# Two feed-forward products of a decoder layer by seven products of quarters in place of eight

## The chip, the core and the metric
One core of a Trainium2 chip runs one program. The metric is device microseconds of one execution; lower is better.

## The reference
One layer over 1032 tokens (1024 of a prompt, 8 sampled), all in float32. Three head groups give `mix`; then

```
x = x + mix @ w_out                                   # 1024 x 1024
h2 = rms_norm(x, norm2_g)
x = x + square(relu(h2 @ w_ff1)) @ w_ff2              # 1024 -> 4096 -> 1024
```

## The kernel before
Features lie on the partitions, tokens along the free dimension. A float32 factor is split into a high part, rounded to the matmul's type, and a low part (`split`, lines 108 to 114: a cast on ACT, then a subtraction on DVE or POOL). `dense` (146 to 154) makes three matmuls of each 128-row tile: high by high, high by low, low by high. Tokens go in three groups of 344 (`TG`). `split`, `add`, `mul`, `sub` are helpers, so the profile shows DVE and POOL operations at L51, ACT's at L71 or L74, matmuls at L83, loads at L80.

`merge` (1168) loads the eight tiles of `mix` from memory and splits them. `out_proj` (1180) runs over eight output tiles `d`: one weight unit (`wunit`, two halves of 128x512), 72 matmuls, the residual added, the result stored to `x1s`, and its scaled, split form kept in `xg`; its squares are summed into `r2`. `ffn` (1211) takes `ff1(m)` for 32 tiles of the hidden layer (72 matmuls, relu, square, split into `hb`) and, after every fourth, `ff2(fb)`, which adds four hidden tiles' part to eight output tiles `ya`; the last round multiplies by `r2`, adds `x1s` and stores. So 64 units of 72 matmuls of 344 columns run there; each weight half is split by ACT and POOL, and results leave PSUM through DVE or ACT. The whole of the former `ffn` stands in the diff below with a minus.

A scheduler puts each engine's instructions in an order when the program is built; pools and their buffer counts decide what may run ahead. DMAs of these parts are issued by SP in its order.

## Time and profile before

| | us |
|---|---|
| three runs | 1544.86, 1545.30, 1550.38 |
| median | 1545.3 |
| profiled execution, span of its instructions | 1548.3 |
| PE busy in it | 1452.3 (94%) |
| DVE, ACT, POOL busy | 756.9, 459.7, 488.8 |

The page lists no time of the profiled execution beside its span, which lies 3.0 us above the median and within the three runs. Durations below are of that execution. A busy share says little by itself: what ends last in a stage is read from the chain and the waits there.

### The profile page before, as it was taken

The page shows a single profiled execution, that of the slowest core. Times are in us where ns is not written, and L with a number is a line of the kernel's source. Part 1 is how long each engine was busy: PE and PEld are TensorE (multiplying, and loading weights), DVE is VectorE, ACT ScalarE, POOL GpSimd, SP SyncE. Part 2 cuts the span into 40 slices and gives each one's busy share as a digit, 9 for nine tenths or more (in the row PEclk, how much of TensorE's full clock was granted, in tenths as well). Part 3 has the DMA queues.
Part 4 walks back from the last instruction along what each step waited for, and adds up shares of the span by engine and source line. Part 5 has one row for each costly group of instructions (what it writes and reads, how often), then busy time and mean ns, then how long its engine had stood idle before and what let it go on. Part 6 is the DMA issues. An engine that isn't in the chain of part 4 may idle for free.

```text
span 1548.3 us, 26824 instructions
## 1 busy us (share of the span) xinstructions
PE 1452.3 (94%) x10623; PEld 1348.1 (87%) x10623; DVE 756.9 (49%) x1690; ACT 459.7 (30%) x1012; POOL 488.8 (32%) x762
## 2 busy tenths in 40 slices
PE   5899899989898698898999999999999999999998
PEld 5888787879777467566999999999999999999998
DVE  7658467667757655875435203223232322323248
ACT  6433223223223143344433333131221312122130
POOL 7013574461242645440232222222221222222121
PEclk9899899899788577679999999999999999999999
DMA  6153323323435531237432111111111111111125
GB/s 232 60 171 114 91 67 104 98 62 109 125 105 127 156 77 43 82 98 252 153 121 82 55 41 50 47 46 51 41 55 41 48 49 41 55 41 49 48 66 180
DMA packets 102264, 136.87 MB, mean 88 GB/s; under 512 B 36115, under 2 KB 58604, under 8 KB 101996
## 3 DMA queue, kind: packets, MB, share of 16 engines
q1 hardware_dynamic: 96924, 128.61, 25.8%
q0 software_dynamic: 5216, 6.56, 2.0%
q8 instruction: 83, 1.36, 0.3%
q14 instruction: 41, 0.34, 0.1%
HBM read 102.07 MB, written 34.10 MB: 88 GB/s over the span
## 4 chain that ended last, share of the span: by engine, by line
PE 76%; DVE 8%; DMA 5%; POOL 5%; issue 3%; ACT 2%; SPq 1%; ACTq 0%; POOLq 0%; DVEq 0%
PE d L83 38%; PE g L83 33%; POOL inv L51 4%; PE cx L83 2%; PE cy L83 2%; DMA qs<-xs 2%; PE g L87 1%; SPq L80 1%; DVE F L51 1%; DMA mst<-mixs 1%; DMA W<-ws 1%; DMA ws<-inv 1%; DVE hbig L68 1%; DMA kn<-kvs 1%; DVE xs L68 0%
## 5 line engine op out<-in xcount | busy, mean ns | idle before, releaser
L83 PE MATMUL d<-xg,w 128*128 128x344 f32 x2304 | 366.1, 320 | 0.0
L83 PEld LDWEIGHTS d<-xg,w 128*128 128x128 f32 x2304 | 363.9, 188 | 0.9 <-ACT rel L71 0.3
L83 PE MATMUL g<-hb,w 128*128 128x344 f32 x2304 | 364.2, 320 | 0.0
L83 PEld LDWEIGHTS g<-hb,w 128*128 128x128 f32 x2304 | 363.1, 188 | 0.0
L51 POOL TENSOR_TENSOR w<-wf,w 128x512 fp32r<-128x512 f32 x130 | 169.6, 1305 | 553.5 <-ACT w L74 553.5
L83 PE MATMUL d<-hbig,w 128*128 128x344 f32 (+2 forms) x1296 | 227.7, 333 | 18.2 <-ACT w L74 9.5
L83 PEld LDWEIGHTS d<-hbig,w 128*128 128x128 f32 x1296 | 207.6, 205 | 33.0 <-ACT w L74 10.7
L74 ACT CAST w<-wf 128x512 fp32r<-128x512 f32 x190 | 117.5, 619 | 334.7 <-PE g L83 263.1
L51 DVE TENSOR_TENSOR ya<-g,ya 128x344 f32<-128x344 f32 x168 | 86.6, 515 | 187.4 <-PE g L83 187.3
L51 DVE TENSOR_TENSOR rel<-rel 128x344 f32<-128x344 f32 x96 | 49.5, 516 | 243.7 <-ACT rel L71 243.7
L71 ACT ACTIVATE rel<-d 128x344 f32<-128x344 f32 x96 | 43.9, 458 | 193.7 <-PE d L83 192.5
L51 DVE TENSOR_TENSOR hb<-rel,hb 128x344 fp32r<-128x344 f32 x96 | 70.9, 739 | 53.0 <-ACT hb L74 53.0
L51 POOL TENSOR_TENSOR inv<-inv,blk 128x54 f32<-128x54 f32 (+24 forms) x217 | 71.7, 330 | 53.8 <-DMA out_state_p<-sl 20.5
L51 POOL TENSOR_TENSOR inv<-inv,inv 128x54 f32<-128x54 f32 (+24 forms) x217 | 74.9, 345 | 15.9
L74 ACT CAST hb<-rel 128x344 fp32r<-128x344 f32 x96 | 46.0, 480 | 38.6 <-DVE rel L51 36.1
L51 DVE TENSOR_TENSOR w<-wf,w 128x512 fp32r<-128x512 f32 x60 | 42.3, 705 | 30.5 <-ACT w L74 29.6
L83 PE MATMUL d<-mix,w 128*128 128x344 f32 x288 | 51.2, 327 | 2.8 <-ACT mix L74 2.4
L83 PEld LDWEIGHTS d<-mix,w 128*128 128x128 f32 x288 | 45.9, 190 | 7.2 <-ACT mix L74 3.2
L51 POOL TENSOR_TENSOR r<-r,osq 128x344 f32<-128x344 f32 x21 | 24.5, 1170 | 86.2 <-ACT r L71 46.5
L71 ACT ACTIVATE xs<-pr,omm 128x344 f32<-128x344 f32 x42 | 24.5, 583 | 86.8 <-DVE pr L51 50.8
L83 PE MATMUL g<-mix,w 128*128 128x344 f32 x288 | 49.7, 323 | 0.0
L83 PEld LDWEIGHTS g<-mix,w 128*128 128x128 f32 x288 | 46.5, 190 | 0.2 <-issue 0.2
(370 smaller groups left out, 1861.2 us busy)
## 6 DMA issues: line engine op xcount, KB each, us to landing
wf<-in_w_ff SPq DMA_DIRECT2D x128, 256.0 KB
wf<-in_w_in SPq DMA_DIRECT2D x34, 256.0 KB
tmp<-xs SPq DMA_DIRECT2D x32, 256.0 KB
x<-in_xT SPq DMA_DIRECT2D x8, 516.0 KB
xs<-xs SPq DMA_DIRECT2D x24, 172.0 KB
xr<-in_xT SPq DMA_DIRECT2D x8, 516.0 KB
x1s<-xr SPq DMA_DIRECT2D x8, 516.0 KB
x<-x1s SPq DMA_DIRECT2D x8, 516.0 KB
```

The lines of the kernel that those rows point to most:

```text
L51: return (e or self.nc.vector).tensor_tensor(out, a, b, op=op)
L68: return self.nc.vector.scalar_tensor_tensor(out, a, s, b, op0=op0, op1=op1)
L71: return self.nc.scalar.activation(out, a, f, **k)
L74: return self.nc.scalar.copy(out, a)
L80: return self.nc.sync.dma_start(out=out, in_=a)
L83: return self.nc.tensor.matmul(out, l, r, start=start, stop=stop, **k)
L87: return self.nc.tensor.transpose(out, a, ident)
```

## The change
Both products are cut into quarters: hidden or output rows by halves, inner dimension by halves, tokens into two halves of 516 (`TH`), each of two groups of 258 columns (`TQ2`). Seven products of sums and differences of quarters (forms) give the four results. `w_forms` makes seven split forms of a unit's four raw 128x512 pieces: four DVE subtractions, seven casts on ACT, seven on POOL to finish the split. `x_early` and `x_late` make the token forms, `h_forms(c)` seven forms of 128x1032 from the hidden tiles, which now go to memory (`hs`) and come back. `product` has a PSUM tile of two banks, four in turn. `up(j, ws)` replaces `ff1` (16 steps of seven products of 24 matmuls), `down(c, o, ws, hf)` replaces `ff2` (8 rounds `c` of 4 outputs `o`, seven products of 12 matmuls each, added into six `acc` tiles). The weight forms have 7 buffers (tags `w`, `w2`), the hidden forms 8 (`xy`, `xe`), raw hidden tiles and their sums 8 (`t4`). `merge` and `out_proj` take `t4` tiles for their loads, and `out_proj` goes by pairs 0, 4, 1, 5 and so on. Some small constants lie in another pool.

```diff
+            self.ea = ctx.enter_context(pool("early_forms", L))
             with pool("mix", L) as self.fp:
                 self.merge()
                 self.out_proj()
-            with pool("ff", L) as self.fp:
-                self.ffn()
-            xgp.__exit__(None, None, None)
+            self.eb = ctx.enter_context(pool("late_forms", L))
+            psp.__exit__(None, None, None)
+            self.psp = ctx.enter_context(self.tc.tile_pool(name="psum2", bufs=2, space=PSUM))
+            self.ffn()
...
+    def t4(self):
+        return self.xgp.tile([128, T], F32, name=self.nm("t4"), tag="t4", bufs=8)
+    def hx(self, n=TH):
+        return self.ea.tile([128, TH], F32, name=self.nm("st"), tag="st", bufs=5)[:, :n]
...
-            f = self.fp.tile([128, TP], F32, name=self.nm("mst"), tag="mst", bufs=2)
-            self.dma(f, self.mixs[k])
+            f = self.t4()
+            self.dma(f[:, :TP], self.mixs[k])
...
-        for d in range(8):
+        self.x1 = [None] * 8
+        self.xf = [[None, None] for _ in range(7)]
+        for n, d in enumerate((0, 4, 1, 5, 2, 6, 3, 7)):
             w = self.wunit(I["w_out"][d])
-            xr = fp.tile([128, T], F32, name=self.nm("xr"), tag="xres", bufs=2)
+            xr = self.x1[d] = self.t4()
...
-            x = self.xgp.tile([128, 2, T], F32R, name=f"xg{d}")
-            self.split(x[:, 0], x[:, 1], xr, scale=v[:, V_G2 + d:V_G2 + d + 1])
-            self.xg.append((x[:, 0], x[:, 1]))
...
+            self.act(xr, xr, AF.Copy, scale=v[:, V_G2 + d:V_G2 + d + 1])
+            if n % 2:
+                self.x_early(n // 2)
...
+    def form(self, tile, k, x, e=None):
+        self.split(tile[:, 0, k], tile[:, 1, k], x, e=e)
+    def xt(self, i, half):
+        tag, n = (("xy", 4), ("xe", 4), ("xf", 6))[min(i // 2, 2)]
+        pool = self.ea if i < 4 else self.eb
+        self.xf[i][half] = pool.tile([128, 2, 2, TH], F32R, name=self.nm(tag), tag=tag, bufs=n)
+        return self.xf[i][half]
...
+    def x_early(self, k):
+        half = k // 2
+        b11, b12, b21, b22 = self.x_quads(k)
+        g = self.nc.gpsimd
+        if k % 2 == 0:
+            for i in range(4):
+                self.xt(i, half)
+        f = [self.xf[i][half] for i in range(4)]
+        self.form(f[0], k % 2, b11, g)
+        self.form(f[1], k % 2, b21, g)
+        t1 = self.hx()
+        self.sub(t1, b12, b11)
+        t2 = self.hx()
+        self.sub(t2, b22, t1)
+        self.form(f[2], k % 2, t2)
+        self.form(f[3], k % 2, t1)
+    def x_late(self):
+        g = self.nc.gpsimd
+        for i in (4, 5, 6):
+            for half in range(2):
+                self.xt(i, half)
+        f = lambda i, k: (self.xf[i][k // 2], k % 2)
+        for k in range(4):
+            b11, b12, b21, b22 = self.x_quads(k)
+            t3 = self.hx()
+            self.sub(t3, b22, b12)
+            self.form(*f(4, k), t3)
+        for k in range(4):
+            self.form(*f(5, k), self.x_quads(k)[3], g)
+        for k in range(4):
+            b11, b12, b21, b22 = self.x_quads(k)
+            u, t3 = self.hx(), self.hx()
+            self.sub(u, b21, b11)
+            self.sub(t3, b22, b12, g)
+            self.sub(u, u, t3)
+            self.form(*f(6, k), u)
+    def w_raw(self, src):
+        self.nwf = getattr(self, "nwf", 0) + 1
+        pool, tag, n = ((self.wp, "wf", 2), (self.eb, "wf2", 4))[self.nwf % 3 > 0]
+        raw = pool.tile([128, 512], F32, name=self.nm(tag), tag=tag, bufs=n)
+        self.dma(raw, src)
+        return raw
+    def w_form(self, x, e):
+        self.nwt = getattr(self, "nwt", 0) + 1
+        pool, tag, n = ((self.wp, "w", 4), (self.eb, "w2", 3))[self.nwt % 7 > 3]
+        w = pool.tile([128, 2, 512], F32R, name=self.nm(tag), tag=tag, bufs=n)
+        self.split(w[:, 0], w[:, 1], x, e=e)
+        return w
+    def w_forms(self, a11, a12, a21, a22):
+        g, v = self.nc.gpsimd, self.nc.vector
+        a11, a12, a21, a22 = (self.w_raw(x) for x in (a11, a12, a21, a22))
+        sx = lambda: self.hx(512)
+        r = [self.w_form(a11, g), self.w_form(a12, g)]
+        s1, s2 = sx(), sx()
+        self.add(s1, a21, a22, v)
+        self.sub(s2, s1, a11, v)
+        r += [self.w_form(s2, g), self.w_form(s1, g)]
+        s3 = sx()
+        self.sub(s3, a11, a21, v)
+        r.append(self.w_form(s3, g))
+        s4 = sx()
+        self.sub(s4, a12, s2, v)
+        return r + [self.w_form(s4, g), self.w_form(a22, g)]
+    def product(self, ws, xs):
+        out = self.psp.tile([128, 2, 512], F32, name=self.nm("pq"), tag="pq", bufs=4)
+        n = len(ws) * 3
+        for g in range(2):
+            i = 0
+            for (a, c), (hi, lo) in zip(ws, xs):
+                for l, r in ((a, hi), (a, lo), (c, hi)):
+                    self.mm(out[:, g, :TQ2], l, r[:, g * TQ2:g * TQ2 + TQ2], start=i == 0, stop=i == n - 1)
+                    i += 1
+        return out[:, :, :TQ2]
     def ffn(self):
-        nc, fp, I = self.nc, self.fp, self.I
-        hb = fp.tile([128, 6, 2, T], F32R, name="hb")
-        ya = fp.tile([128, 8, T], F32, name="ya")
-        def ff1(m):
-            w = self.wunit(I["w_ff1"][m], nc.gpsimd)
-            for t0, tn in TG:
-                p = self.ps("d")
-                self.dense(p[:, :tn], w, 0, self.xg, t0, tn)
-                r = fp.tile([128, 344], F32, name=self.nm("rel"), tag="rel", bufs=2)
-                self.act(r, p[:, :tn], AF.Relu)
-                self.mul(r, r, r)
-                self.split(hb[:, m % 6, 0, t0:t0 + tn], hb[:, m % 6, 1, t0:t0 + tn], r)
-        def ff2(fb):
-            last = fb == 7
-            hs = [(hb[:, m % 6, 0], hb[:, m % 6, 1]) for m in range(4 * fb, 4 * fb + 4)]
-            for dp in range(4):
-                w = self.wunit(I["w_ff2"][fb, dp], nc.gpsimd)
-                for d2 in range(2):
-                    d = dp * 2 + d2
-                    if last:
-                        x1 = fp.tile([128, T], F32, name=self.nm("x1"), tag="xres", bufs=2)
-                        self.dma(x1, self.x1s[d])
-                    for t0, tn in TG:
-                        p = self.ps("g")
-                        self.dense(p[:, :tn], w, d2 * 512, hs, t0, tn)
-                        y = ya[:, d, t0:t0 + tn]
-                        if fb == 0:
-                            self.cp(y, p[:, :tn])
-                        else:
-                            self.add(y, p[:, :tn], y)
-                        if last:
-                            self.mul(y, y, self.r2[:, t0:t0 + tn])
-                            self.add(y, y, x1[:, t0:t0 + tn])
-                    if last:
-                        self.dma(self.O["yT"][:, d], ya[:, d])
-        for fb in range(8):
-            for j in range(4):
-                ff1(fb * 4 + j)
-                if j == 0 and fb:
-                    ff2(fb - 1)
-        ff2(7)
+        nc, I = self.nc, self.I
+        two = lambda x: x.rearrange("p (g n) -> p g n", g=2)
+        self.hs = self.dp.tile([32, 128, T], F32, name="hs")
+        def up(j, ws):
+            xs = [[(f[k // 2][:, 0, k % 2], f[k // 2][:, 1, k % 2]) for k in range(4)] for f in self.xf]
+            w = [[(f[:, 0, k * 128:k * 128 + 128], f[:, 1, k * 128:k * 128 + 128]) for k in range(4)] for f in ws]
+            pp, h1, h2 = self.t4(), self.t4(), self.t4()
+            p1, u2, c11, c12, c21, c22 = (two(x[:, s * TH:s * TH + TH]) for x in (pp, h1, h2) for s in range(2))
+            def square(h, m):
+                self.stt(h, h, 0.0, h, ALU.max, ALU.mult)
+                self.mul(h, h, self.r2)
+                self.dma(self.hs[m], h)
+            p = self.product(w[0], xs[0])
+            self.cp(p1, p)
+            p = self.product(w[1], xs[1])
+            self.add(c11, p, p1)
+            p = self.product(w[2], xs[2])
+            self.add(u2, p, p1)
+            p5 = self.product(w[3], xs[3])
+            self.add(c12, p5, u2)
+            p = self.product(w[4], xs[4])
+            self.add(c21, p, u2)
+            self.add(c22, p5, c21)
+            p = self.product(w[5], xs[5])
+            self.add(c12, p, c12)
+            square(h1, j)
+            p = self.product(w[6], xs[6])
+            self.add(c21, p, c21)
+            square(h2, j + 16)
+        w1 = lambda j: self.w_forms(*(I["w_ff1"][m][:, i * 512:i * 512 + 512] for m in (j, j + 16) for i in range(2)))
+        w2 = lambda c, u: self.w_forms(*(I["w_ff2"][c, u, q] for q in range(4)))
+        ws = w1(0)
+        self.x_late()
+        for j in range(16):
+            nxt = w1(j + 1) if j < 15 else w2(0, 0)
+            if j == 15:
+                hf = self.h_forms(0)
+            up(j, ws)
+            ws = nxt
+        acc = [self.eb.tile([128, 4, TH], F32, name=f"acc{i}", tag="xf", bufs=6) for i in range(6)]
+        def down(c, o, ws, hf):
+            k0 = (o % 2) * 2
+            xs = [[(f[:, 0, k], f[:, 1, k]) for k in range(2)] for f in hf]
+            w = [[(f[:, 0, k * 128:k * 128 + 128], f[:, 1, k * 128:k * 128 + 128]) for k in range(k0, k0 + 2)] for f in ws]
+            c11, u2, u4, u3, p3, p4 = (x[:, o] for x in acc)
+            def to(out, p, first=True):
+                if c == 0 and first:
+                    self.cp(two(out), p)
+                else:
+                    self.add(two(out), p, two(out))
+            last = c == 7
+            g = nc.gpsimd
+            if c == 2 + o:
+                x1 = []
+                for d in (o, o + 4):
+                    x = self.t4()
+                    self.dma(x, self.x1s[d])
+                    x1 += [x[:, :TH], x[:, TH:]]
+                self.add(c11, c11, x1[0], g)
+                self.add(p4, p4, x1[2], g)
+                self.add(u4, u4, x1[3], g)
+                self.add(p3, p3, x1[1], g)
+                self.sub(p3, p3, x1[3], g)
+            put = lambda d, t, y: self.dma(self.O["yT"][:, d, t * TH:t * TH + TH], y)
+            p = self.product(w[0], xs[0])
+            to(c11, p)
+            to(u2, p)
+            p = self.product(w[1], xs[1])
+            to(c11, p, False)
+            if last:
+                put(o, 0, c11)
+            to(u2, self.product(w[2], xs[2]), False)
+            to(u4, self.product(w[3], xs[3]))
+            if last:
+                self.add(u4, u4, u2)
+                self.add(p3, p3, u4, g)
+                self.add(p4, p4, u2, g)
+            to(u3, self.product(w[4], xs[4]))
+            if last:
+                self.add(u4, u4, u3)
+                put(o + 4, 1, u4)
+                self.add(p4, p4, u3)
+            to(p3, self.product(w[5], xs[5]))
+            if last:
+                put(o, 1, p3)
+            to(p4, self.product(w[6], xs[6]))
+            if last:
+                put(o + 4, 0, p4)
+        for c in range(8):
+            for o in range(4):
+                if o % 2 == 0:
+                    nxt = w2(c, 1) if o == 0 else w2(c + 1, 0) if c < 7 else None
+                if o == 1 and c < 7:
+                    nhf = self.h_forms(c + 1)
+                down(c, o, ws, hf)
+                if o % 2:
+                    ws = nxt
+            if c < 7:
+                hf = nhf
+    def h_forms(self, c):
+        g, v = self.nc.gpsimd, self.nc.vector
+        q = []
+        wide = lambda: self.t4().rearrange("p (j n) -> p j n", j=2)
+        for f in range(2):
+            for t in range(2):
+                x = wide()
+                for j in range(2):
+                    self.dma(x[:, j], self.hs[f * 16 + 2 * c + j, :, t * TH:t * TH + TH])
+                q.append(x)
+        b11, b12, b21, b22 = q
+        r = []
+        def put(x, e):
+            n = c * 7 + len(r)
+            f = self.ea.tile([128, 2, 2, TH], F32R, name=self.nm("hf"), tag=("xy", "xe")[n % 8 // 4], bufs=4)
+            self.split(f[:, 0], f[:, 1], x, e=e)
+            r.append(f)
+        put(b11, g)
+        put(b21, v)
+        t1, t2, t3, t4 = (wide() for _ in range(4))
+        self.sub(t1, b12, b11, v)
+        self.sub(t2, b22, t1, v)
+        put(t2, g)
+        put(t1, v)
+        self.sub(t3, b22, b12, g)
+        put(t3, v)
+        put(b22, g)
+        self.sub(t4, b21, t2, v)
+        put(t4, v)
+        return r
```

Three places of the order. First DVE: before, in a round of `ff2` (`ya` the output sum, `g` a PSUM tile), only results out of PSUM, and an `ff1` square:

```order
L51 TENSOR_TENSOR ya_8636<-g_1637_12575,ya_8636 128x344
L51 TENSOR_TENSOR ya_8636<-g_1638_12589,ya_8636 128x344
L51 TENSOR_TENSOR ya_8636<-g_1639_12603,ya_8636 128x344
L51 TENSOR_TENSOR rel_1645_12652<-rel_1645_12652 128x344
L51 TENSOR_TENSOR hb_8635<-rel_1645_12652,hb_8635 128x344
```

Now, where `down(3, 3)` ends and `down(4, 0)` begins (`pq` a PSUM product, `acc` the sums, `t4` raw hidden tiles and their sums, `hf` a form, `st` a weight sum):

```order
L53 TENSOR_TENSOR t4_1936_14164<-t4_1931_14149,t4_1930_14146 128x1032
L53 TENSOR_TENSOR acc4_12466<-pq_1906_13982,acc4_12466 128x516
L53 TENSOR_TENSOR acc5_12467<-pq_1907_13996,acc5_12467 128x516
L53 TENSOR_TENSOR hf_1871_13673<-t4_1866_13656,hf_1871_13673 128x1032
L53 TENSOR_TENSOR st_1914_14024<-wf2_1910_14014,wf_1911_14016 128x512
L53 TENSOR_TENSOR t4_1937_14165<-t4_1933_14155,t4_1936_14164 128x1032
L53 TENSOR_TENSOR acc0_12462<-pq_1923_14047,acc0_12462 128x516
L53 TENSOR_TENSOR acc1_12463<-pq_1923_14047,acc1_12463 128x516
L53 TENSOR_TENSOR st_1915_14025<-st_1914_14024,wf_1908_14010 128x512
L53 TENSOR_TENSOR st_1918_14034<-wf_1908_14010,wf2_1910_14014 128x512
L53 TENSOR_TENSOR t4_1939_14167<-t4_1932_14152,t4_1937_14165 128x1032
L53 TENSOR_TENSOR acc2_12464<-pq_1926_14090,acc2_12464 128x516
```

Subtractions between SBUF tiles have come ahead of the results of `pq_1923`, the first product of the new round.

POOL, before, at any place of the feed-forward part:

```order
L51 TENSOR_TENSOR w_1623_12436<-wf_1622_12434,w_1623_12436 128x512
L51 TENSOR_TENSOR w_1631_12525<-wf_1630_12523,w_1631_12525 128x512
L51 TENSOR_TENSOR w_1633_12530<-wf_1632_12528,w_1633_12530 128x512
L51 TENSOR_TENSOR w_1641_12619<-wf_1640_12617,w_1641_12619 128x512
L51 TENSOR_TENSOR w_1643_12624<-wf_1642_12622,w_1643_12624 128x512
```

Now, over the same boundary: the seven splits `w`, `w2` of one weight set, with three splits `hf` and a subtraction of 1032 columns among and behind them:

```order
L53 TENSOR_TENSOR w_1883_13783<-wf2_1879_13775,w_1883_13783 128x512
L53 TENSOR_TENSOR hf_1867_13659<-t4_1864_13654,hf_1867_13659 128x1032
L53 TENSOR_TENSOR w_1884_13786<-wf_1880_13777,w_1884_13786 128x512
L53 TENSOR_TENSOR w_1887_13793<-st_1886_13790,w_1887_13793 128x512
L53 TENSOR_TENSOR w2_1888_13796<-st_1885_13789,w2_1888_13796 128x512
L53 TENSOR_TENSOR hf_1870_13669<-t4_1860_13644,hf_1870_13669 128x1032
L53 TENSOR_TENSOR w2_1890_13801<-st_1889_13799,w2_1890_13801 128x512
L53 TENSOR_TENSOR w2_1892_13806<-st_1891_13804,w2_1892_13806 128x512
L53 TENSOR_TENSOR w_1893_13809<-wf2_1882_13781,w_1893_13809 128x512
L53 TENSOR_TENSOR hf_1934_14158<-t4_1930_14146,hf_1934_14158 128x1032
L53 TENSOR_TENSOR t4_1938_14166<-t4_1933_14155,t4_1931_14149 128x1032
```

POOL's subtractions of 128x1032 now stand between weight splits, one of them ahead of the second weight form.

SP at the end of the sampled tokens' attention, before (`d4` its loads, `mst` the mixed tokens):

```order
L80 DMA d4_1128_7699<-in_mem_v 128x4x256
L80 DMA mst_1139_7773<-mixs_71 128x1024
L80 DMA d4_1129_7705<-in_mem_v 128x4x256
L80 DMA mst_1140_7777<-mixs_71 128x1024
L80 DMA d4_1130_7711<-in_mem_v 128x4x256
L80 DMA mst_1141_7781<-mixs_71 128x1024
```

Now:

```order
L82 DMA d4_1129_7705<-in_mem_v 128x4x256
L82 DMA mixs_71<-ao_1114_7640 128x512
L82 DMA d4_1130_7711<-in_mem_v 128x4x256
L82 DMA d4_1131_7717<-in_mem_v 128x4x256
L82 DMA t4_1134_7757<-mixs_71 128x1024
L82 DMA t4_1135_7761<-mixs_71 128x1024
```

The loads of the mixed tokens have moved behind the last load of that attention.

## Rows read from the trace of the kernel before

**Rows 1.** the profile's page: span, engine shares, PE and clock by slice.
```profile
span 1548.3 us, 26824 instructions
...
PE 1452.3 (94%) x10623; PEld 1348.1 (87%) x10623; DVE 756.9 (49%) x1690; ACT 459.7 (30%) x1012; POOL 488.8 (32%) x762
...
PEclk9899899899788577679999999999999999999999
...
GB/s 232 60 171 114 91 67 104 98 62 109 125 105 127 156 77 43 82 98 252 153 121 82 55 41 50 47 46 51 41 55 41 48 49 41 55 41 49 48 66 180
```

**Rows 2.** windows; columns: us, busy us and count by engine, PEclk, DMA share, GB/s.
```profile
821.00:1545.00 724.00, 721.77 (x4577) 721.12 (x4575) 237.65 (x411) 173.08 (x340) 160.91 (x124) 1.00 0.17 55
```

**Rows 3.** chain that ended last, in order of time: start us, us, what.
```profile
873.16 45.28 PE g L83 x288
...
1497.38 45.41 PE g L83 x288
...
1543.91 0.52 DVE ya L51
```

**Rows 4.** groups of PE by form; columns: names, shape, count, busy us, mean ns, idle.
```profile
L83 PE MATMUL d<-xg,w 128*128 128x344 f32 x2304 | 366.1, 320 | 0.0
```

**Rows 5.** timeline of PE, 360 to 475 us; columns: start us, us, what.
```profile
364.50 3.81 PE L83 MATMUL d<-hbig,w 128*128 128x256 f32 x30
...
415.10 3.57 PE L83 MATMUL d<-hbig,w 128*128 128x256 f32 x15 [4.28 <-DVE stat L77]
```

**Rows 6.** timeline of PE, 388 to 400 us, and one matmul's own length (tile hbig).
```profile
387.76 2.17 PE L83 MATMUL d<-hbig,w 128*128 128x256 f32 x17
...
L83 PE MATMUL d<-hbig,w x353: 274/283/682, 359.7 to 473.6; 128*128 128x256 f32 x132, 128*128 128x264 f32 x36, 128*128 128x344 f32 x9
```

**Rows 7.** groups of DVE by form.
```profile
L51 DVE TENSOR_TENSOR ya<-g,ya 128x344 f32<-128x344 f32 x168 | 86.6, 515 | 187.4 <-PE g L83 187.3
...
L51 DVE TENSOR_TENSOR F<-cx,F 128x512 f32<-128x512 f32 x16 | 11.0, 688 | 19.1 <-PE cx L83 19.0
...
L68 DVE SCALAR_TENSOR_TENSOR xg<-xr,vec,xg 128x1032 fp32r<-128x1032 f32 x8 | 10.4, 1298 | 3.7 <-ACT xg L71 3.7
```

**Rows 8.** groups of ACT by form.
```profile
L74 ACT CAST w<-wf 128x512 fp32r<-128x512 f32 x190 | 117.5, 619 | 334.7 <-PE g L83 263.1 <-PE d L83 58.6 <-DMA wf<-in_w_in 6.1
```

**Rows 9.** groups of POOL by form.
```profile
L51 POOL TENSOR_TENSOR w<-wf,w 128x512 fp32r<-128x512 f32 x130 | 169.6, 1305 | 553.5 <-ACT w L74 553.5
...
L51 POOL TENSOR_TENSOR d<-d,t 128x1024 f32<-128x1024 f32 x3 | 7.5, 2496 | 0.0
```

**Rows 10.** timeline of POOL, 8 to 44 us.
```profile
15.41 2.29 POOL L51 TENSOR_TENSOR w<-wf,w 128x512 fp32r<-128x512 f32 x1
...
19.89 3.42 POOL L51 TENSOR_TENSOR acc<-acc,sq 128x1032 f32<-128x1032 f32 x1
...
28.91 12.01 POOL L51 TENSOR_TENSOR macc<-macc,msq 128x256 f32<-128x256 f32 x7
```

**Rows 11.** timeline of DVE, 8 to 44 us.
```profile
16.48 2.31 DVE L51 TENSOR_TENSOR acc<-acc,sq 128x1032 f32<-128x1032 f32 x1
18.72 5.68 DVE L68 SCALAR_TENSOR_TENSOR hbig<-x,vec,hbig 128x1032 fp32r<-128x1032 f32 x2
...
35.87 2.45 DVE L68 SCALAR_TENSOR_TENSOR ml<-mT,vec,mh 128x256 fp32r<-128x256 f32 x6
```

**Rows 12.** chain, 690 to 830 us, at the mixed tokens' loads.
```profile
715.18 6.71 DMA mst<-mixs
```

**Rows 13.** timeline of PE, 700 to 760 us, and of 814 to 822 us.
```profile
736.79 0.60 PE L87 MATMUL cy<-cst,t 128*128 128x128 f32 x4
...
813.77 0.64 PE L83 MATMUL g<-mix,w 128*128 128x344 f32 x3
...
814.56 1.68 PE L83 MATMUL d<-xg,w 128*128 128x344 f32 x8
```

**Rows 14.** chain of the whole span: one weight load on it.
```profile
87.10 2.60 DMA wf<-in_w_in
```

More of the change, by code (lines that the diff above doesn't have):

```diff
@@ L20 @@
 TG = [(0, 344), (344, 344), (688, 344)]
+TH = T // 2
+TQ2 = TH // 2
 CW = math.exp(-0.5)
@@ L160, in build @@
             self.wp = tp("w")
-            self.psp = tp("psum", 2, space=PSUM)
+            psp = self.tc.tile_pool(name="psum", bufs=2, space=PSUM)
+            self.psp = psp.__enter__()
             self.dp = tp("dram", 1, space=DRAM)
@@ L182, in consts @@
         t = lambda n, s, d=F32: self.cpool.tile(s, d, name=n, tag=n)
+        tr = lambda n, s, d=F32: self.rp.tile(s, d, name=n, tag=n)
         self.cst = t("cst", [128, NCST])
@@ L1193, in out_proj @@
             self.dma(self.x1s[d], xr)
-            x = self.xgp.tile([128, 2, T], F32R, name=f"xg{d}")
-            self.split(x[:, 0], x[:, 1], xr, scale=v[:, V_G2 + d:V_G2 + d + 1])
-            self.xg.append((x[:, 0], x[:, 1]))
-            if d == 0:
+            if n == 0:
                 self.act(acc, xr, AF.Square)
             else:
-                for t0, tn in TG:
-                    sq = fp.tile([128, 344], F32, name=self.nm("osq"), tag="osq", bufs=2)
-                    self.act(sq, xr[:, t0:t0 + tn], AF.Square)
-                    self.add(acc[:, t0:t0 + tn], acc[:, t0:t0 + tn], sq, nc.gpsimd)
-        self.r2 = acc
+                for h in range(2):
+                    sq = self.hx()
+                    sl = slice(h * TH, h * TH + TH)
+                    self.act(sq, xr[:, sl], AF.Square)
+                    self.add(acc[:, sl], acc[:, sl], sq, nc.gpsimd)
+            self.act(xr, xr, AF.Copy, scale=v[:, V_G2 + d:V_G2 + d + 1])
+            if n % 2:
+                self.x_early(n // 2)
         for t0, tn in TG:
```

38 lines of the change are left out of this document (19 added, 19 removed).

## The prediction

> **What bounds it now.** I read the page first, then the windows, the chain, the groups by form and the timelines. On the page PE is busy 94% of the span and the granted clock reads 9 in every slice of the second half [rows 1]; in the feed-forward window PE is busy 721.77 of 724.00 us at clock 1.00, while DVE has 237.65, ACT 173.08 and POOL 160.91 [rows 2]. The chain there is PE alone, in pieces of 288 matmuls; after its last matmul come three short DVE operations, the last at 1543.91, and a store [rows 3]. So the part from 814.56 us [rows 13] to the end of the last piece, 1497.38 + 45.41 = 1542.79 [rows 3], is a queue of 4608 matmuls of 344 columns (two groups of 2304 [rows 4]), and every other engine has room. The change takes columns from PE and gives forms to the engines with room. The question is whether they have it where it is wanted.
>
> **PE.** A piece of 288 in 45.4 us is 157.7 ns a matmul [rows 3]; the mean of 320 ns in the group [rows 4] overlaps its neighbours and is no price. Removed: 4608 x 0.1577 = 726.7 us. Added: up, 16 steps x 7 products x 24 = 2688; down, 8 rounds x 4 outputs x 7 x 12 = 2688; 5376 matmuls of 258 columns. The nearest rows have 256: 30 of them in 3.81 us, less one's own 0.28 [rows 6], give 3.53/29 = 122 ns [rows 5]; 17 in 2.17 give 1.89/16 = 118 [rows 6]. I take 120: 645.1 us. PE gains 82 (71 to 92 with the ends).
>
> The Trainium skill ("TensorE: Matmul & The Clock Gate", Back-to-back issue gap) gives N/2.4 + 2.5 ns at full clock, so 110 at 258 columns and 591 us, an estimate that would gain 54 more. By it 344 columns would take 146; the row says 157.7, so the trace does not agree, and the sum goes by the rows.
>
> **Prices elsewhere.** DVE: 0.69 us for 512 columns [rows 7], the same for 516; a result out of PSUM with an SBUF operand costs this too (0.515 at 344); 1032 columns, from 1.298 for one with a scale, I take as 1.24. POOL: 1.30 for 512, 2.4 for 1032 (2.496 at 1024 with waits in it) [rows 9]. ACT: 0.62 for 512 [rows 8]. DVE and POOL do not add up freely. At startup a DVE operation of 1032 columns takes 2.31, and two of the next take 5.68, while POOL's 512-column split takes 2.29 and its 1032-column sum 3.42 [rows 10, 11]: each waits for the other. From 16.48 to 18.72 one of each passes, 2.24 us for 1.24 + 1.30 = 2.54, so taking turns costs about 0.88 of the sum. The results out of PSUM are not touched by this (0.515 over 168, POOL at work beside many) [rows 7].
>
> **Up, per step**: PE 168 x 0.120 = 20.2. DVE 7 results (4.8), 4 weight sums (2.8), 4 square operations of 1032 (5.0) = 12.6; POOL 7 x 1.30 = 9.1; ACT some 5. The turns take 0.88 x (2.8 + 5.0 + 9.1) = 14.9. All lies beside PE: 0. If each of DVE's eight shared operations waits for two thirds of a POOL split, 0.9, DVE needs 12.6 + 8 x 0.9 = 19.8, so the cover is thin; 0 to +10.
>
> **Down, per round**: PE 336 x 0.120 = 40.3, for 45.4 before. DVE 32 results (22.1), 8 weight sums (5.5), 7 operations of 1032 for the hidden forms (8.7): 36.3. POOL 14 weight splits (18.2) and 4 of 1032 (9.6): 27.8, with 6.5 more in rounds 2 to 5 for the five residual sums. Shared: 14.2 + 27.8 = 42.0. By the sums it nearly fits, but the work is not spread. Seven weight buffers hold one set and eight hidden forms one set and one more: the next forms can be written only as the last output's products finish, and are wanted seven products later. In DVE's order the four splits, `t1`, `t2`, `t4` and three weight sums stand ahead of results that PE waits for, PSUM holding four products. Take the time from the start of a round's last output. PE wants to start the sixth product of the next round after 12 products, 17.3 us; for that the second product's result must have left PSUM. Ahead of it stand 10 shared DVE operations, 7 x 1.24 + 3 x 0.69 = 10.8, and POOL's 7 splits and four of 1032, 18.7. In turns: 0.88 x 29.5 = 26.0, after 2.1 until the first form may be written, and 1.4 for two results: 29.5. PE loses 12.2 there. It loses in lumps: after an idle 4.28 us, 15 matmuls took 3.57 [rows 5], (3.57 - 0.28)/14 = 235 ns, the lower clock level, 1.7 us more than at 120; two lumps make 3.4. I take 15 per boundary, six times, and 5 at the last, where no further forms are made (18.9 in turns): **+95**. Ends: DVE alone, waiting for no one, reaches that result at 20.5, so 3.2 a boundary, +22; with the residual sums (2.3), and `t1` behind a reload that waits for POOL's sixth split (about 3, a load [rows 14]), 20 to 22, +130.
>
> **The edges.** The mixed tokens' loads go behind the attention's last loads. Before, part of the out-projection ran among them; a load there took 6.71 us in company [rows 12] and the attention's last PE work stands at 736.79 [rows 13]. Without that company the attention may end up to 14 us sooner (two loads of 6.71), so the loads start between 723 and 738; eight of 512 KB at the page's best slice, 252 GB/s [rows 1], take 16.6, a split 2.3; 105 matmuls can run meanwhile, the other 471 x 0.158 = 74.4 follow. End 816 to 831 for 814.4: +9 (+2 to +17). The first weight set waits for buffers under the mixed tokens: load 2.60 [rows 14], cast 0.62, split 1.30: +5. `x_late` has 20 DVE operations (13.8) and 8 on POOL (10.4) beside the first set (11.9): 0.88 x 36 = 32 until the last form; product seven could start at 22, and the next step's first products fill a part: +7 (0 to +20). From up to down, the first hidden forms add 18.3 of shared work to a step of 20: +5 (0 to +10). The end has one DVE operation for three: -1.
>
> Sum: -82 + 0 + 95 + 9 + 5 + 7 + 5 - 1 = +38. Against 1548.3 that is 1586; the median lies 3.0 below the span, so **1583 us**, 2.4% slower. Its own range, with boundaries of 10 to 20 us (-30, +35) and half of the other ends, is 1540 to 1632.
>
> **Rivals.**
> *The forms hide* (faster). DVE and POOL find gaps, and a boundary costs DVE's own 3.2: 1583 - 73 = 1510. For it: the sums of a round nearly fit, and results out of PSUM leave POOL free. Against it: [rows 10, 11]. It needs under 5 us a boundary. 0.27.
> *DVE keeps the turn.* Six DVE operations in a row took 2.45 us while POOL's seven small sums stretched over 12.01 [rows 10, 11]: POOL waited, DVE did not. Half of the six boundaries' 90 goes: 1583 - 45 = 1538. Against it: the long operations took turns strictly. 0.10.
> *Full blocking* (slower). No 0.88: six boundaries lose 3.5 more, and the start 4: 1608. The Trainium skill ("SBUF — State Buffer", Who interferes with whom) says that the later of the two blocks fully; the rows show some overlap. 0.10.
> *The issue floor* (slower). Not columns but weight loads set the interval, 157.7 for 5376: 848 us, and 1583 + 203 less what then hides, 95: 1690. Against it: [rows 5, 6]. 0.03.
> *The page's gap of 110 ns.* Up would be held by DVE's 19.8 a step (6 us less), down by the turns (nothing): 1577. 0.03.
> That the work shrinks as said is in the order: 5376 matmuls of 258 columns.
>
> **How the numbers follow.** The forecast has 0.47, with the slower rivals 0.63. A measurement tells some 0.5% from no change, so no change is 1537.6 to 1553.0: DVE keeping the turn gives 0.07 there and 0.03 below. Faster is 0.27 + 0.03 = 0.30. The range, 1500 to 1632, takes in the hidden forms and leaves out the issue floor and the ends' extremes.
>
> **What would show it.** Right: PE about 119 ns apart in up with no waits, idle PE or a lower clock at each round's beginning, DVE and POOL operations of 1032 columns near the sum of two, results of the new round late behind `t2` and `t4`. Wrong: a down round near 41 us, or DVE idle while PE waits.

## The result, and the profile after

The changed kernel took 1611.42 us in the median of four runs (1598.54 to 1618.97) against 1545.08 (1543.08 to 1550.38): ratio 1.0415, 95% interval 1.0365 to 1.0465. It is slower, as forecast, and by 66 us between the medians where 38 were forecast. The profiled execution took 1609.69, its span is 1607.9, 59.6 more than before, and the account below is made of that.

The page of the changed kernel, engines and slices; the clock of its second half is to be held against [rows 1]:

```profile
span 1607.9 us, 29328 instructions
...
PE 1399.0 (87%) x11391; PEld 1289.4 (80%) x11391; DVE 1145.0 (71%) x1914; ACT 508.9 (32%) x1009; POOL 846.7 (53%) x927
...
PE   5998989989786897979987999999978877887798
...
PEclk9999998899897687678998999999989998988899
```

PE's slices in the kernel before:

```profile
PE   5899899989898698898999999999999999999998
```

Before, PE read 9 in every slice of the second half but the last, and the clock 9 in all. Now both read 9 in the first half of the feed-forward part (up, slices 23 to 29); in the second (down, from slice 30) PE reads 7 or 8 in all slices but one, and the clock 8 or 9.

Windows of the changed kernel (columns as in [rows 2]): steady up, rounds 1 to 6 of down (rounds are counted from 0), the first 25 us of round 3, and the rest of it:

```profile
860.00:1145.00 285.00, 282.11 (x2325) 281.31 (x2325) 208.02 (x222) 70.10 (x117) 167.60 (x101) 0.99 0.33 111
1228.10:1556.00 327.90, 264.90 (x2018) 260.35 (x2017) 276.62 (x281) 91.72 (x132) 235.02 (x129) 0.90 0.27 84
1336.40:1361.40 25.00, 13.79 (x86) 13.18 (x85) 23.25 (x18) 2.01 (x4) 20.31 (x10) 0.73 0.26 83
1361.40:1391.60 30.20, 30.20 (x254) 30.20 (x254) 24.43 (x30) 12.74 (x19) 20.77 (x15) 1.00 0.35 110
```

In up PE is busy 282 of 285. In this round of down it loses everything in the first 25 us (86 matmuls, granted clock 0.73, DVE busy 23.25 and POOL 20.31 of 25) and nothing afterwards (30.20 of 30.20, clock 1.00). What it waits for there, in the timeline of PE:

```profile
1340.30 3.11 PE L85 MATMUL pq<-hf,w 128*128 128x258 f32 x24 [0.84 <-DVE acc L53]
1349.38 2.92 PE L85 MATMUL pq<-hf,w 128*128 128x258 f32 x12 [5.96 <-DVE acc L53]
1356.70 35.47 PE L85 MATMUL pq<-hf,w 128*128 128x258 f32 x279 [4.40 <-DVE acc L53]
```

Each wait ends with a result (`acc`) on DVE, and the 12 matmuls between two of them take (2.92 - 0.28)/11 = 240 ns apiece, the lower level of the clock (1.2 GHz). Why the results come late stands in the timelines of the other two engines, first DVE:

```profile
1340.68 3.46 DVE L53 TENSOR_TENSOR hf<-t,hf 128x1032 fp32r<-128x1032 f32 x1
1344.07 1.75 DVE L53 TENSOR_TENSOR st<-wf,wf 128x512 f32<-128x512 f32 x1
1345.74 2.29 DVE L53 TENSOR_TENSOR t<-t,t 128x1032 f32<-128x1032 f32 x1
1347.95 1.28 DVE L53 TENSOR_TENSOR acc<-pq,acc 128x516 f32<-128x516 f32 x2
1349.15 2.88 DVE L53 TENSOR_TENSOR st<-st,wf 128x512 f32<-128x512 f32 x1
1351.96 2.84 DVE L53 TENSOR_TENSOR st<-wf,wf 128x512 f32<-128x512 f32 x1
```

POOL over the same stretch:

```profile
1340.65 2.41 POOL L53 TENSOR_TENSOR hf<-t,hf 128x1032 fp32r<-128x1032 f32 x1
1343.01 3.92 POOL L53 TENSOR_TENSOR w<-st,w 128x512 fp32r<-128x512 f32 x2
1346.90 2.25 POOL L53 TENSOR_TENSOR w<-wf,w 128x512 fp32r<-128x512 f32 x1
1349.12 2.38 POOL L53 TENSOR_TENSOR hf<-t,hf 128x1032 fp32r<-128x1032 f32 x1
1351.45 2.81 POOL L53 TENSOR_TENSOR t<-t,t 128x1032 f32<-128x1032 f32 x1
```

The hidden split takes 3.46 in place of 1.24, a weight sum of 512 columns 2.88 in place of 0.69 [rows 7]: each starts as one POOL operation ends (1340.68, 1349.15), stands while POOL's next one takes its full time (2.41, 2.38), and ends 1.1 and 0.55 after that. The two results between them take 1.28, undisturbed. From 1340.65 to 1354.8 DVE's five shared operations, those with both inputs in SBUF (2 x 1.24 + 3 x 0.69 = 4.55), and POOL's six (3 x 2.4 + 3 x 1.30 = 11.1) ran in 14.15 us, 0.90 of their sum of 15.65; the prediction took 0.88.

Where the 59.6 us went, from the starts of the first matmul of each step (168 matmuls) and round (336):

| stretch | time | at 120 ns | lost | forecast |
|---|---|---|---|---|
| to the first product | 827.96, before 814.56 | | 13.4 | 9 + 5 |
| up, steps 0 and 1 | 35.4, 25.6 | 40.3 | 20.7 | 7 |
| up, steps 2 to 14 | 262.1: 20.6, then 20.1 each | 262.1 | 0 | 0 |
| up, step 15, and down, round 0 | 29.0, 48.0 | 60.5 | 16.5 | 5 |
| down, rounds 1 to 6 | 54.0 to 55.2 | 40.3 each | 86.1 | 90 |
| down, round 7 | 47.4 | 40.3 | 7.1 | 5 |
| after the last matmul | 4.5, before 5.5 | | -1.0 | -1 |

Lost in all 142.8. The old matmuls had taken 728.2 (814.56 to 1542.79), the new ones take 645 at 120 ns, 83 less; the difference, 59.7, is the 59.6.

### The profile page after: what moved, and what is told of

The parts are those of the page before. It is cut to its first block, busy times and chain, and to the rows that moved or that the text cites. A ratio compares the mean times of both kernels' runs of the same rounds, so it can differ in the third digit from the quotient of the medians.

```text
span 1607.9 us, 29328 instructions
## 1 busy us (share of the span) xinstructions
PE 1399.0 (87%) x11391; PEld 1289.4 (80%) x11391; DVE 1145.0 (71%) x1914; ACT 508.9 (32%) x1009; POOL 846.7 (53%) x927
## 5 line engine op out<-in xcount | busy, mean ns | idle before, releaser
L85 PE MATMUL pq<-hf,w 128*128 128x258 f32 x2688 | 351.3, 295 | 72.2 <-DVE acc L53 69.0
L85 PEld LDWEIGHTS pq<-hf,w 128*128 128x128 f32 x2688 | 345.5, 201 | 77.9 <-issue 66.9
L53 POOL TENSOR_TENSOR w<-st,w 128x512 fp32r<-128x512 f32 x128 | 212.6, 1672 | 89.3 <-ACT w L76 88.5
L53 DVE TENSOR_TENSOR acc<-pq,acc 128x516 f32<-128x516 f32 x232 | 153.2, 686 | 54.9 <-PE pq L85 54.2
L85 PE MATMUL pq<-xf,w 128*128 128x258 f32 x1152 | 147.6, 289 | 20.0 <-ACT t L76 17.0
L85 PEld LDWEIGHTS pq<-xf,w 128*128 128x128 f32 x1152 | 144.5, 196 | 21.4 <-ACT t L76 17.4
L53 DVE TENSOR_TENSOR st<-wf,wf 128x512 f32<-128x512 f32 x64 | 74.9, 1171 | 46.4 <-DMA wf<-in_w_ff 34.9
L85 PE MATMUL pq<-xy,w 128*128 128x258 f32 x768 | 97.8, 287 | 0.9 <-DVE r L67 0.7
L85 PEld LDWEIGHTS pq<-xy,w 128*128 128x128 f32 x768 | 95.8, 193 | 2.3 <-ACT xy L76 1.7
L85 PE MATMUL pq<-xe,w 128*128 128x258 f32 x768 | 94.8, 282 | 0.0
L85 PEld LDWEIGHTS pq<-xe,w 128*128 128x128 f32 x768 | 93.3, 189 | 0.0
```

Source lines behind the costliest of these rows:

```text
L53: return (e or self.nc.vector).tensor_tensor(out, a, b, op=op)
L85: return self.nc.tensor.matmul(out, l, r, start=start, stop=stop, **k)
```

## The experiments

Three questions: what makes a boundary of down (the beginning of a round) cost 14 us, what would take it away, and what holds the start of the feed-forward part. Runs of either kernel scatter by up to 1.3%, so an experiment on a boundary is read from its rounds, from first matmul to first matmul, 54.7 in the mean of rounds 1 to 6 of the changed kernel and 40.3 without loss; totals of one run stand beside them.

**1. A boundary without GpSimd's splits of the weights.** The low parts of the weight forms are left out in down.

```diff
-        self.split(w[:, 0], w[:, 1], x, e=e)
+        self.cp(w[:, 0], x)
...
-        w = [[(f[:, 0, ...], f[:, 1, ...])
+        w = [[(f[:, 0, ...], f[:, 0, ...])
```

> In the down rounds the low parts of the seven weight forms of a set are not made (TensorE reads the high part again in their place), so GpSimd loses its 14 operations of 512 columns a round and keeps four of 1032; TensorE, VectorE and the number of buffers stay as they are, and VectorE still has three subtractions, four splits and three or four weight sums among the results at a boundary. Turns theory (VectorE and GpSimd wait for each other): shared work ahead of the second product's result falls from 10.8 + 18.7 to 10.8 + 9.6, in turns 0.88 x 20.4 = 18.0, with 2.1 and 1.4 around it 21.5, 4.2 after TensorE wants it, some 6 with one lump at the lower clock: rounds of 46 in place of 54.5, VectorE's 1032-column operations back near 1.24 where GpSimd is idle, total near 1545. Buffer theory (eight form buffers hold one set and one form, so the forms come too late whoever makes them): rounds stay at 54, total 1608. Order theory (the subtractions and sums that stand ahead of the results cost their own 1.24 and 0.69, whatever GpSimd does): rounds at 43 to 44 here too, but then VectorE's operations must have been near 1.24 before.

1558.64 in one run; rounds 1 to 6 took 47.0 to 48.9, 47.9 in the mean. A boundary fell from 14.3 to 7.6, with not one buffer more: want of buffers alone does not make the forms late. 6.7 of the 14.3 were these 14 splits.

**2. Nor its splits of the hidden forms.**

```diff
+            if e is v:
                 self.split(f[:, 0], f[:, 1], x, e=e)
+            else:
+                self.cp(f[:, 0], x)
...
-        self.sub(t3, b22, b12, g)
-        put(t3, v)
+        put(b22, v)
```

> As the variant without the low parts of the weight forms in down, and now also without GpSimd's three splits and one subtraction of the hidden forms (TensorE reads the high part again; the fifth form is made of the second half of the tokens alone): GpSimd has nothing but the residual sums in down, VectorE's work is what it was. This parts a boundary's 14 into what GpSimd's turns cost and what VectorE's own order costs. The prediction's lower end had 3.2 for VectorE alone, with a lump at the lower clock 1.7 more: turns theory: rounds of 43.5 to 45, VectorE's 1032-column operations at 1.24, total near 1520 to 1532. Order theory: no less than the 47 to 49 that the variant without the weights' low parts had, total 1558.

1510.43 in one run; rounds 1 to 6 took 42.0 to 43.1, 42.5 in the mean. VectorE's groups in those rounds (columns: count, busy us, mean ns, idle before):

```profile
L53 DVE TENSOR_TENSOR acc<-pq,acc 128x516 f32<-128x516 f32 x190 | 126.3, 691 | 39.4 <-PE pq L85 38.4
L53 DVE TENSOR_TENSOR hf<-t,hf 128x1032 fp32r<-128x1032 f32 x26 | 31.9, 1226 | 0.0
L53 DVE TENSOR_TENSOR t<-t,t 128x1032 f32<-128x1032 f32 x16 | 19.7, 1228 | 1.8 <-DMA wf<-in_w_ff 1.1 <-DMA t<-hs 0.6
```

The same groups in rounds 1 to 6 of the changed kernel:

```profile
L53 DVE TENSOR_TENSOR acc<-pq,acc 128x516 f32<-128x516 f32 x190 | 125.5, 686 | 45.4 <-PE pq L85 44.8
L53 DVE TENSOR_TENSOR hf<-t,hf 128x1032 fp32r<-128x1032 f32 x25 | 48.3, 1934 | 0.4 <-ACT hf L76 0.4
L53 DVE TENSOR_TENSOR t<-t,t 128x1032 f32<-128x1032 f32 x18 | 39.2, 2178 | 0.1
```

The same operations take 1.23 alone and 1.93 to 2.18 beside GpSimd; the results take 0.69 in both. Of a boundary's 14.3 VectorE's own order costs 2.2 and GpSimd's turns 12; the round of 42.5 lies a little under the 43.5 to 45 that were expected. The scheduler sets the order anew for each kernel, so the rows of VectorE do not stand in the very same order in these runs; the kind and number ahead of the results stayed, three or four splits, three subtractions and three or four sums.

**3. VectorE's three subtractions later.**

```diff
+        with self.tc.issue_after(self.late.ins) if c else ExitStack():
             self.sub(t1, b12, b11, v)
             self.sub(t2, b22, t1, v)
```

> The three subtractions of VectorE for the forms of the round after next are put behind the last result of the new round's first output; nothing else changes. Turns theory: three of the ten shared operations leave the stretch, they and GpSimd's turn between them, 3 x 2.3 = 6.9 as the trace has them, less what the next waits take over: rounds of 48 to 51, total 1570 to 1590. Buffer theory: the forms are no earlier, rounds stay at 54, total 1608.

1576.24 in one run; rounds 1 to 6 took 45.0 to 50.0 but for one of 55.4, 49.6 in the mean: the turns theory again. In the round of 55.4 the second output took 18.5: there, it seems, what was put off came due.

**4. GpSimd's share of the hidden forms to VectorE.**

```diff
-        g, v = self.nc.gpsimd, self.nc.vector
+        g = v = self.nc.vector
```

> All four of GpSimd's 1032-column operations of the hidden forms (three splits, one subtraction) go to VectorE, 1.24 each in place of 2.4. Turns theory: shared work ahead of the second product's result is 10.8 + 3 x 1.24 on VectorE and 18.7 - 3 x 2.4 on GpSimd, 0.88 x 26.0 = 22.9 in place of 26.0: rounds of 51 to 52, total 1585 to 1595. If VectorE's own queue is what binds and GpSimd lies beside it, four more operations make rounds 3.7 to 5 longer: 58 to 60, total 1635 to 1650.

1591.94 in one run; rounds 1 to 6 took 49.8 to 54.4, 51.5 in the mean. VectorE gets 32 operations more and the rounds get shorter: what counts is the sum over both engines, and an element costs VectorE half of what it costs GpSimd (1.24 and 2.4 for 1032 columns).

**5. More buffers and with them another order, the work the same.**

```diff
-        return self.xgp.tile([128, T], F32, name=..., tag="t4", bufs=8)
+        return self.xgp.tile([128, T], d, name=..., tag="t4", bufs=25)
...
-            f = self.ea.tile([128, 2, 2, TH], F32R, ..., bufs=4)
-            self.split(f[:, 0], f[:, 1], x, e=e)
+            hi, lo = raw(), raw()
+            self.split(hi, lo, x, e=e)
```

> High and low part of a form get a buffer of 128x1032 each, out of one stock of 25 with the hidden loads and differences, so that three of the next round's seven forms can be made in the course of a round; the subtractions come first; the first hidden forms are written behind up's last step, the residual loads ahead of a round. The work is the same. Buffer theory: the last four forms have three more products of time, boundaries nearly vanish: rounds of 41 to 43, total 1500 to 1515. Turns theory: three forms and three subtractions leave the boundary, 0.88 x (2 x 1.24 + 2.4 + 3 x 1.24 + 2.4) = 9.7 less of shared work ahead, boundaries of 3 to 5: rounds of 43 to 46, total 1515 to 1540. If the sum over a round binds (22.1 of results, 14.2 of VectorE's and 27.8 of GpSimd's shared work), rounds stay above 48, total over 1560.

1569.28, ratio to before 1.0125 (1.0100 to 1.0151). Rounds 1 to 6 took 45.5 to 50.1, 48.1 in the mean: better than the changed kernel, worse than both the buffer theory and my turns figure (43 to 46), and at the edge of the third case. The forms now lie all over the round, the waits too: several outputs of a round take 11 to 17.7 us where an undisturbed one takes 10.1. DVE is busy 258.51 and POOL 234.32 of 288.30 us. Round 0 took 57.4 for 48.0, and step 15 21.9 for 29.0: the loss at that seam only moved.

**6. The loops of down turned, the operations the same.** In a round the products come outermost and the outputs inside. The storage changes with it: differences are made in place, and the raw weights get the buffers of four hidden forms.

```diff
+        order = (0, 1, 5, 4, 2, 3, 6)
+        seq = [(n, i) for n in range(8) for i in order]
+        for q, (n, i) in enumerate(seq):
+            cur = nxt
...
+                nxt = forms(i2, *data[n2], tmp)
+            run(n, i, *cur)
```

> Down keeps its eight rounds, its 256 results, its 1827 operations on VectorE and 906 on GpSimd and who does which; only the loops are turned: in a round the seven products outermost, the four outputs inside, so that a form is made shortly before its product and not all seven at the boundary. Heap theory (the same work in turns fits if it is spread: 22.1 beside, 0.88 x 42 = 37 of 40.3): rounds of 41 to 45, total 1515 to 1550. Sum theory (VectorE's 36.3 and its waits for GpSimd fill a round however they lie): rounds of 47 to 52, total 1560 to 1595, and the turned-round kernel with pairs of rounds owes its time to having half the results.

1572.01 in one run. The rounds took 57.1, 44.1, 48.3, 51.7, 52.0, 52.0, 40.7 and 40.8. Both theories hold, each in its place. Round 6 makes all forms for round 7, has no residual sums and takes 40.7: spread out, the same forms cost nothing there. In rounds 1 to 5 GpSimd also adds the residual (20 sums, 1.30 alone, 1.658 here). With five of them (6.5) the sum in turns is 0.88 x 48.5 = 42.7, 2.4 over the round's 40.3, but rounds 2 to 5 lost 8.0 to 11.7: the sum says that such a round overflows, not by how much. Nor is the residual shown to be what tips it: round 1 loses its 3.8 before its first residual sum, and round 6 also loads next to nothing (DMA busy share 0.01, in rounds 1 to 5 0.27 to 0.33). No run took either out alone.

**7. Loops turned and the sum made smaller.** Pairs of rounds add up in PSUM, which halves the results, and VectorE takes the low parts of two weight forms in seven and all hidden ones.

```diff
-        for c in range(8):
-            for o in range(4):
+        seq = [(n, i) for n in range(4) for i in order]
...
+                for c in range(2):
+                    f, w = hf[c], wf[c * 2 + o // 2]
...
+    return v if i in (1, 4) else g
```

> Down is turned round: four groups of two rounds, in a group the seven products outermost and the four outputs inside, so that a form is made shortly before its product, used for four outputs and given up, and TensorE adds up two rounds in PSUM: 128 results of 516 columns in place of 256. All low parts of the hidden forms go to VectorE (1.24), as do those of the weights of two of the seven products; the other 20 of a group's 28 stay with GpSimd. By the prices a group (TensorE 80.6) has 22.1 of results, 8 x 1.24 = 9.9 of differences, 14 x 1.24 = 17.4 of splits, 16 x 0.69 of weight sums and 8 x 0.69 of weight splits on VectorE, 66 in all, and 26 of GpSimd's splits. Turns theory, shared work heaped at the boundary being the loss: nothing is heaped any more, shared work is 0.88 x (43.9 + 26) = 61.5 under 80.6, a group takes 81 to 84, the start of down some 10: total 1515 to 1535. If the sum of shared work and results binds wherever it lies (66 + 26 = 92 a group), groups take 88 to 95: 1550 to 1580, hardly under the variant with more buffers (1569).

1523.75, ratio to before 0.9823 (0.9767 to 0.9879): faster than both kernels. The groups of two rounds took 87.7, 85.3, 82.6 and 84.8 where TensorE alone takes 80.6 and 81 to 84 were expected. Its down as a window:

```profile
1176.20:1516.60 340.40, 327.43 (x2688) 325.58 (x2688) 278.97 (x301) 128.42 (x184) 186.49 (x104) 0.98 0.34 113
```

That of the changed kernel:

```profile
1180.10:1603.40 423.30, 351.14 (x2690) 345.40 (x2688) 349.50 (x358) 120.27 (x178) 291.90 (x163) 0.90 0.27 86
```

The same 2688 matmuls are through in 340.4 in place of 423.3, with the clock at 0.98 in place of 0.90. The turned loops, the halved results and the shares of the engines came together here, so the gain is not divided among them.

**8 and 9. The start: the norm later, the token forms in place.** On the changed kernel, then on the one of experiment 7.

```diff
+            if j == 0:
+                self.norm()
             square(h1, j)
...
-            t3 = self.hx()
-            self.sub(t3, b22, b12)
-            self.form(*f(4, k), t3)
+            self.sub(b12, b22, b12)
+            self.form(*f(4, k), b12)
```

> The changed kernel but for the start of the feed-forward part: the three matmuls and reciprocals of the norm come after the sixth product of the first step in place of before the first, and the last token forms are made in place, without the second copy of a difference on GpSimd. The start cost 13.4 us before the first product and 20.6 in the first two steps. Theory (the first product waits for the norm, and the token forms for VectorE, which does reciprocals of 2.3 and shares its turns with GpSimd): the first product 5 to 7 us earlier, the first two steps 6 to 12 us shorter, total 1590 to 1597. Rival (the first step waits for buffers alone: products one to four fill PSUM and the fifth waits until a token buffer comes free, which the order of VectorE's work sets): the first product earlier by the same, the first two steps as before or longer, total 1601 to 1606.

> The turned-round down and the changed start together. If the two losses are independent, the gains add: the total lies below the turned-round kernel's by as much as the changed start lies below 1608 (10 to 18 us by the theory, 2 to 7 by the rival); 1500 to 1525, 1 to 3% under the kernel before.

1605.65 and 1523.71 (0.9823, 0.9775 to 0.9870): next to nothing. The total of the first is the rival's, but not for its reason: the first product came no earlier, at 827.63 where it had come at 827.96. With the norm gone from in front of it, it waited for a weight form instead, in the timeline of PE of the second of these kernels (its out-projection ended some 7 us later in that run):

```profile
834.63 1.32 PE L85 MATMUL pq<-xy,w 128*128 128x258 f32 x4 [5.99 <-ACT w L76]
838.95 7.46 PE L85 MATMUL pq<-xy,w 128*128 128x258 f32 x44 [3.00 <-POOL w L53]
```

The cast and the split of the first weights stood behind the last token forms on ACT and POOL.

**10. The order at the start set by hand, on the kernel of experiment 9.**

```diff
+            for x in self.first + [self.s2i]:
+                q.enter_context(self.tc.issue_after(x.ins))
+            self.x_late()
...
+                with self.tc.issue_after(self.lastmm.ins):
+                    self.norm()
```

> The turned-round kernel with the changed start, and the order at the start set by hand: the last token forms behind the first two weight forms and the second weight sum on each engine, the norm's matmuls behind the sixth product's. The first product should then not wait for the norm nor for the weights' low part: first product 3 to 8 us after the out-projection's last matmul in place of 6.7 to 10, the first three steps 72 to 78 in place of 79 to 85, total 1508 to 1518. If the start is bound by the sum of forms whatever their order, it stays at 1521 to 1526.

1516.33, ratio 0.9812 (0.9775 to 0.9849), the fastest kernel that leaves nothing out, though its interval and that of experiment 7 overlap widely. The first product came 2.4 us after the out-projection, but the first three steps took 81.2 where 72 to 78 were expected: the time won was lost again before the fifth product, in one wait of 12.64 us for a copy on ACT.

**11 and 12. What that copy waits for.** VectorE's last token differences go behind the fifth form; then, in a second kernel, a ninth token buffer too.

```diff
-            self.sub(b21, b21, b11)
+            with self.tc.issue_after(lo):
+                self.sub(b21, b21, b11)
```
```diff
-tag="t4", bufs=8
+tag="t4", bufs=9
```

> The kernel with the start set by hand, and now VectorE's last differences of the tokens (for the seventh form) behind the low parts of the fifth form. There the first three steps took 81.2, with one gap of 12.9 before the fifth product, where eight differences in a row took 13.7 on VectorE and the first product's copy out of PSUM waited for a token buffer. Forms theory (the fifth product waits for its form): the form is complete some 4 to 6 us earlier and the gap shrinks by as much, the first step 35 to 37 in place of 41.0, total near 1511. Buffer theory (PSUM is full and the copy waits for a token buffer, which only the last differences free): the gap stays at 12 to 15, the first step 40 to 44, total 1516 to 1519.

> As the run before, with a ninth token buffer, so that the first product can leave PSUM at once. Buffer theory: the gap before the fifth product falls to 6 to 9 (what the form itself takes), and a second wait of some us may come behind it, where the second product's result wants a buffer: the first step 35 to 38, total 1509 to 1513. Forms theory: no difference to the run before.

1522.40 (0.9829, 0.9788 to 0.9869) and 1527.15 (0.9850, 0.9813 to 0.9887). The waits before the fifth product, in the timelines of PE: first with the order alone:

```profile
857.74 8.13 PE L85 MATMUL pq<-xf,w 128*128 128x258 f32 x48 [17.82 <-ACT t L76]
```

With the ninth buffer as well:

```profile
844.22 1.01 PE L85 MATMUL pq<-xf,w 128*128 128x258 f32 x3 [4.14 <-DVE xf L53]
```

The form was ready sooner, the differences that give up a buffer came later, and the wait grew from 12.64 to 17.82: it was for the buffer. With a ninth one the first product left PSUM at 833.75 and the fifth began at 839.79, for which it then waited piecemeal, for its forms: step 0 took 43.8, after 46.4 with the order alone and 41.0 without it. So the buffer holds the fifth product here, and right behind it stand the forms: with the buffer given, step 0 came to 43.8 and not to the 35 to 38 that the buffer theory expected. Neither kernel beats experiment 10.

## Why the prediction was right, and where it was too small

**PE: right.** 5376 matmuls at 120 ns were taken; 12 of the 16 steps of up took 20.1 us, 119.6 ns a matmul, and so did every undisturbed output of down (10.1 for 84). The 110 ns by the formula of the Trainium skill ("TensorE: Matmul & The Clock Gate", Back-to-back issue gap), which stands there for an isolated matmul, do not show at 258 columns either.

**Up hides its forms: right.** No wait in steps 3 to 14, DVE busy 208.02 and POOL 167.60 of 285. The 0 held; the +10 kept for it was not needed.

**Boundaries, +95: right, in size, place and mechanism.** Measured 86.1 + 7.1 = 93. The step that carries it was "In turns: 0.88 x 29.5 = 26.0" and "PE loses 12.2 there", with 3.4 for two lumps at the lower clock. In rounds 1 to 6 the gaps over 0.4 us sum to 10.1 to 11.9 and the rest to 2.8 to 4.0. Experiment 2 shows the cause by taking GpSimd out (14.3 to 2.2); VectorE alone had been put at 3.2, by a 20.5 that the prediction does not work out. Experiments 1, 3 and 4 came out at 47.9, 49.6 and 51.5 where the same arithmetic gave 46, 48 to 51 and 51 to 52. Where the work was spread over the round, the arithmetic was too low: 43 to 46 for the 48.1 of experiment 5, 41 to 45 for the 48.1 that rounds 1 to 6 of experiment 6 took in the mean. So it is borne out for work heaped ahead of a result, and not for a whole round.

**The rivals.** "The forms hide" needed under 5 us a boundary; it fails in this order of the loops, and it is what happens in round 6 of experiment 6. "DVE keeps the turn" fails: in the stretch above the operations alternate. "Full blocking" would have been the sum itself, and 18.5 a boundary; 0.90 of the sum and 14.3 were measured. That its total, 1608, lies nearest to the measured one is luck: the missing time was lost elsewhere, as told below. The Trainium skill ("SBUF — State Buffer", Who interferes with whom) has an exclusive lock, on which the later engine blocks fully. For one pair of operations that agrees with the rows (a split of 3.46 beside GpSimd's 2.41); over the stretch of 14.15 us a tenth was saved. The issue floor fails with PE's 119.6.

**The start of the feed-forward part, +9 and +5: 13.4, right in size, the 5 for another reason.** The norm's first matmul, which follows the out-projection, came at 821.64, before at 814.24: 7.4 for the 9. The other 6.0 went otherwise than I thought: the first product did not wait for the weights but for the norm in front of it (waits of 2.34 and 0.70, and six matmuls). Its last four matmuls and the longer wait:

```profile
824.72 2.54 PE L85 MATMUL g<-r,ones 128*128 128x344 f32 x4 [2.34 <-POOL r L53]
```

The weights stood right behind that, as experiments 8 and 9 show. The term is no steady one either: in six more kernels with the same code for this start (experiments 1 to 4, 6 and 7) the first product began between 825.3 and 835.5.

**x_late, +7: the first step that failed; measured 20.7.** I wrote "32 until the last form; product seven could start at 22", as though the products waited for forms. They stopped before that: PSUM holds four products, the first could only leave it into a token buffer (`t4`), and all eight were held by the tokens that `x_late` reads. The row in the changed kernel, product five:

```profile
851.11 2.52 PE L85 MATMUL pq<-xf,w 128*128 128x258 f32 x10 [9.71 <-ACT t L76]
```

Experiments 11 and 12 show that such a wait is for the buffer. I counted the `t4` buffers for the hidden forms and not for the step's own results. The wait is 9.7 of the 20.7; other waits are 3.3, and the remaining 7.7 were matmuls at a lower granted clock (0.86 from 827.9 to 841.4, 0.82 from 851.1 to 863.4, 0.88 from there to 889.0). Nor does the 7 look right for the forms: in experiment 12, which has the buffer and an order set by hand, step 0 still took 43.8.

**From up to down, +5: the second; measured 16.5.** The sum had only the 18.3 of shared work in step 15. The seam has the same wait: `h_forms(0)` stands ahead of step 15 in the program and takes all eight buffers that step 15 needs for its results,

```profile
1170.06 10.19 PE L85 MATMUL pq<-xf,w 128*128 128x258 f32 x72 [7.28 <-ACT t L76]
```

and round 0 pays for weight forms on top. In experiment 1, without the weights' low parts, round 0 took 40.7 and step 15 still 29.6; in experiment 2, without GpSimd's hidden splits too, step 15 took 20.1 and round 0 40.3. That the buffers and not the turns alone make step 15's part is argued from the row and from the start; it was not tried alone here, for experiment 2 also takes one buffer less.

For the span 1586 was forecast and 1607.9 measured, 22 more: 13.7 + 11.5 = 25 from these two terms, less some 2 at the boundaries and 1 elsewhere. The other 6 or 7 us between 1583 and 1611 are no step of the sum: the median had been 3.0 below the profiled span and is now 3.5 above.

## What to carry to other kernels

When VectorE and GpSimd both work out of SBUF, add their work up as on one engine and hold that sum, in the stretch where it is due, against the time that is to hide it. Results out of PSUM were not slowed by GpSimd here and stand outside that sum, but they take VectorE's time too, and a sum that just fits was not enough (experiments 5 and 6). Work that fits in the mean is lost if a loop order makes it due all at once: turn the loop so that a form is made shortly before its use and given up soon after, before buying buffers. And for each product ask where its result goes: a full PSUM with no free buffer behind it stopped TensorE (9.71 us in the first step) as a missing operand does.

## What the runs showed of the hardware

A subtraction of 1032 columns took 1.23 us on VectorE without GpSimd's splits (experiment 2) and 2.18 in the mean beside GpSimd, a GpSimd split of 512 columns 1.30 [rows 9] and 1.77, while results out of PSUM stayed at 0.69 throughout; that was expected. What busy shares alone would not tell: moving four operations a round onto the busier of two engines, VectorE, made a round 3 us shorter (51.5 for 54.7).
